# First MLP pair by plain products, block sums between products, and w_down's transfers spread: one change to a decoder-layer kernel

## The chip, the core and the metric

The kernel runs on one core of a Trainium2 chip. It is one program for a whole decoder layer: SEQ = 1024 tokens, model width 1024, MLP width 2816, everything in float32. The metric is the device time of one execution in microseconds (us), as a median over runs.

## The reference, cut to what matters

The change touches the second half of the layer: the residual after the mixers, the norm, the causal ConvFFN MLP.

```python
h = h + rmsnorm(mixed @ w_o, norm_mix_post)
f = rmsnorm(h, norm_ffn_pre) @ w_up                 # 1024 x 1024 @ 1024 x 5632
f = causal_dwconv(f, conv_ffn) + conv_ffn_b         # 3 taps over tokens, per channel
f_gate, f_val = jnp.split(f, 2, axis=-1)            # 2816 channels each
f = (jax.nn.gelu(f_gate) * f_val) @ w_down          # 2816 x 1024
h = h + rmsnorm(f, norm_ffn_post)
```

Ahead of it lie the input projection, a gated DeltaNet mixer and a sparse-attention mixer, and behind it a gated per-layer embedding. The change leaves those alone.

## The kernel before

**Number format.** Every float32 product is done as three matmuls of a rounded format (float32r): a value is split into a high half (ScalarE copies and rounds it) and a low half (another engine subtracts the high half from the value). `hl` does a split and `mm3` the three matmuls. So a 128-row block of K costs three matmuls, and a "product" below, 512 deep and 512 wide, is 4 x 3 = 12 matmuls of 512 columns.

**Blocks of tokens.** `ffn` goes through the eight blocks of 128 tokens. `product(t, half)` multiplies a block with w_o, three blocks ahead of its use. `post` norms the result, adds `x` and gives `h` (stored as `h1d`); the block is normed again and `turned` transposes it on TensorE and splits it into `mx`. `mx[kh, th]` holds half kh of the 1024 inputs for half th of the tokens; for the second half of the tokens, `mx[0, 1]` holds B12 - B11, not B12 itself.

**The MLP pairs.** w_up is used in 22 pairs of 128 gate and 128 value channels; class `UpProjection` holds them. A pair is a 2x2 block product done with seven products instead of eight (Winograd's form of Strassen): its four weight blocks a11, a12 (gate) and a21, a22 (value) meet B11, B12, B21, B22 and three combinations T2, T3, T4. Products 1, 2, 3 and 5 need `mx` alone. Products 6, 7 and 4 need T2, T3, T4. `sums` makes the weight sums s1 to s4 on VectorE, `ring` splits a weight block into one of four slots (high half on ScalarE, low half on GpSimd), `gate_lo` and `gated` do the convolution taps and the GELU, `keep` stores the activations and, for every second pair, four block sums of two pairs (GpSimd), for `down` is a block product of the same kind. `stores` issues those transfers later, on SyncE's queue.

**The start.** Products 1 and 2 of pairs 0 and 1 run between the last blocks (`under`). Then `rest` calls `combine`, which makes T2, T3 and T4 from `t2s` and `mx` on VectorE, GpSimd and ScalarE, and goes on with product 6 of pair 0.

**The order** within an engine's queue is written by a scheduler at build time, from the order of the program, its own cost model, and the buffers that are free. `behind(ins)` ties each instruction in its block to come after `ins` on that engine's queue. A tile with a tag shares its `bufs` slots with every tile of the same tag, so a new one waits until the older one has been read.

**down** runs seven block products, each eleven steps of 12 matmuls over four banks. `run` issues the loads of w_down's quarters (`load_w`) at given steps, on SyncE's queue, behind the load of that step's activations (`araw`).

## Time and profile before

| | us |
|---|---|
| median of 3 runs (1950.59 to 1951.98) | 1951.12 |
| profiled execution | 1951.64 |
| span of its instructions | 1949.9 |
| TensorE busy | 1839.1 |
| VectorE busy | 1224.2 |
| ScalarE busy | 920.3 |
| GpSimd busy | 711.6 |

The span runs from the first to the last instruction that the profile shows; the execution's own time is 1.7 us longer. Busy time counts an instruction from start to end. Matmuls overlap: one of 512 columns lasts 0.39 us in the rows, but starts come closer than that, so the cost of a matmul is read from the distance of the starts. The engines are PE (TensorE), PEld (its weight loads), DVE (VectorE), ACT (ScalarE), POOL (GpSimd) and SP (SyncE, which issues transfers).

### The profile page before, as it was taken

How to read it: one execution, taken by the hardware profiler on the slowest of the kernel's cores; microseconds unless marked ns; L12 is line 12 of the kernel's file. 1: busy time of each engine (PE TensorE's matmuls, PEld its weight loads, DVE VectorE, ACT ScalarE, POOL GpSimd, SP SyncE). 2: the span in 40 equal slices, each digit the busy share in tenths (PEclk: the TensorE clock that was granted, in tenths of full speed). 3: DMA queues.
4: the chain of work that ended last, by engine and by line, in shares of the span. 5: the costliest groups of instructions: out<-in, count | busy, mean ns of one | idle time of the engine just before them, and what ended most of it. 6: DMA issues, size and time to landing. Idle time of an engine off the chain costs nothing.

```text
span 1949.9 us, 25814 instructions
## 1 busy us (share of the span) xinstructions
PE 1839.1 (94%) x9247; PEld 1528.1 (78%) x9247; DVE 1224.2 (63%) x2347; ACT 920.3 (47%) x1816; POOL 711.6 (36%) x537
## 2 busy tenths in 40 slices
PE   7999989999999999999889949999999999999998
PEld 7888778888888887778778837787787877777786
DVE  4448934432277667766694587777677764868643
ACT  4344223323276667766663334444454544446432
POOL 2132212223122112321162166666666664555200
PEclk9999989999999999999999969999999999999999
DMA  5133333333311010200073212232323257246201
GB/s 166 33 95 103 101 83 93 97 87 95 100 28 34 28 39 28 71 23 23 22 248 121 97 55 81 92 103 88 122 83 103 92 184 259 72 146 208 88 33 43
DMA packets 182622, 178.67 MB, mean 92 GB/s; under 512 B 27549, under 2 KB 133342, under 8 KB 182494
## 3 DMA queue, kind: packets, MB, share of 16 engines
q1 hardware_dynamic: 180272, 170.33, 27.8%
q10 hardware_dynamic: 2222, 6.69, 0.9%
q8 instruction: 73, 1.20, 0.3%
q14 instruction: 55, 0.45, 0.1%
HBM read 132.65 MB, written 44.34 MB: 91 GB/s over the span
## 4 chain that ended last, share of the span: by engine, by line
PE 34%; DVE 5%; POOL 4%; issue 3%; ACT 2%; DMA 2%; SPq 0%; POOLq 0%; ACTq 0%; DVEq 0%
PE q L345 3%; PE q L347 3%; PE q L346 3%; PE n L345 2%; PE n L347 2%; PE n L346 2%; PE pg L347 2%; PE pg L346 2%; PE pg L345 2%; PE pwo L347 1%; PE pwo L345 1%; PE pwo L346 1%; POOL whl L313 1%; POOL wdhl L313 1%; DMA araw<-acts 1%
## 5 line engine op out<-in xcount | busy, mean ns | idle before, releaser
L345 PE MATMUL pj<-uh,whi 128*128 128x512 f32 x640 | 260.0, 407 | 6.0 <-DVE y L524 3.7
L347 PE MATMUL pj<-uh,wlo 128*128 128x512 f32 x640 | 255.2, 399 | 0.0
L346 PE MATMUL pj<-ul,whi 128*128 128x512 f32 x640 | 255.2, 399 | 0.0
L313 POOL TENSOR_TENSOR wlo<-raw,whi 128x1024 fp32r<-128x1024 f32 x48 | 117.3, 2446 | 310.5 <-ACT whi L324 266.6
L313 POOL TENSOR_TENSOR whl<-s,whl 128x512 fp32r<-128x512 f32 x88 | 131.3, 1500 | 57.2 <-ACT whl L1344 57.2
L345 PEld LDWEIGHTS pj<-uh,whi 128*128 128x128 f32 x640 | 121.5, 190 | 33.3 <-ACT yz L562 2.8
L347 PEld LDWEIGHTS pj<-uh,wlo 128*128 128x128 f32 x640 | 121.3, 190 | 29.0
L346 PEld LDWEIGHTS pj<-ul,whi 128*128 128x128 f32 x640 | 121.8, 190 | 25.8
L313 POOL TENSOR_TENSOR whl<-raw,whl 128x512 fp32r<-128x512 f32 x66 | 105.8, 1605 | 58.1 <-ACT whl L1344 55.5
L313 POOL TENSOR_TENSOR wdhl<-wd,wdhl 128x512 fp32r<-128x512 f32 x66 | 98.9, 1507 | 76.1 <-ACT wdhl L1344 74.8
L313 DVE TENSOR_TENSOR whl<-araw,whl 128x512 fp32r<-128x512 f32 x77 | 84.4, 1103 | 56.5 <-ACT whl L1344 54.0
L1226 ACT ACTIVATE Pt<-Pt,nm 128x640 f32<-128x640 f32 (+7 forms) x128 | 93.0, 729 | 36.6 <-DVE nm L1224 36.2
L345 PE MATMUL q<-mxh,whl 128*128 128x512 f32 x264 | 103.8, 396 | 4.1 <-ACT u L106 2.8
L1256 DVE TENSOR_TENSOR Tl<-pt,Th 128x512 fp32r<-128x512 f32 (+1 forms) x152 | 92.4, 616 | 22.1 <-ACT Th L1255 17.9
L346 PE MATMUL q<-mxl,whl 128*128 128x512 f32 x264 | 103.5, 392 | 0.0
L347 PE MATMUL q<-mxh,whl 128*128 128x512 f32 x264 | 102.9, 392 | 0.2 <-POOL whl L313 0.2
L1255 ACT ACTIVATE Th<-pt 128x512 fp32r<-128x512 f32 (+1 forms) x152 | 78.5, 538 | 43.7 <-PE po L1259 33.7
L324 ACT ACTIVATE whi<-raw 128x1024 fp32r<-128x1024 f32 x48 | 50.5, 1052 | 82.8 <-PE pj L346 54.1
L1252 PE MATMUL pt<-ident,Pt 128*128 128x128 f32 x528 | 84.6, 280 | 5.0 <-DVE Tl L1256 3.2
L1294 POOL TENSOR_TENSOR tm<-tm 128x128 f32<-128x128 f32 x32 | 14.7, 459 | 197.2 <-DVE tm L1292 157.4
L126 DVE SCALAR_TENSOR_TENSOR yg<-c,cv,yg 128x511 f32<-128x511 f32 (+1 forms) x88 | 82.0, 936 | 1.0 <-ACT yg L123 0.9
L1344 ACT ACTIVATE whl<-s 128x512 fp32r<-128x512 f32 x88 | 54.7, 624 | 55.8 <-PE n L347 44.1
(533 smaller groups left out, 5181.8 us busy)
## 6 DMA issues: line engine op xcount, KB each, us to landing
raw<-in_w_up SPq DMA_DIRECT2D x44, 512.0 KB
raw<-in_w_in SPq DMA_DIRECT2D x40, 512.0 KB
araw<-acts SPq DMA_DIRECT2D x35, 512.0 KB
acts<-sd SPq DMA_DIRECT2D x44, 256.0 KB
gates_d<-yz SPq DMA_DIRECT2D x40, 256.0 KB
acts<-yv SPq DMA_DIRECT2D x33, 256.0 KB
gt<-gates_d SPq DMA_DIRECT2D x32, 256.0 KB
wd<-in_w_down SPq DMA_DIRECT2D x7, 1024.0 KB
```

The costliest lines, as they stand in the source:

```text
L126: self.body.nc.vector.scalar_tensor_tensor(y, src, w, y, ALU.mult, ALU.add)
L313: return eng.tensor_sub(lo, src, hi.bitcast(F32)).ins
L324: nc.scalar.activation(hi, raw, AF.Copy)
L345: nc.tensor.matmul(ps, lh, rh, start=start, stop=False, skip_group_check=more)
L346: nc.tensor.matmul(ps, lh, rl, start=False, stop=False, skip_group_check=more)
L347: nc.tensor.matmul(ps, ll, rh, start=False, stop=stop, skip_group_check=more)
L1226: nc.scalar.activation(Pt[:, hh, 0:nk], Pt[:, hh, 0:nk], AF.Exp, scale=2.0 ** -(h0 + hh + 1), bias=nm[:, br, hh:hh + 1], accum_out=rs[:, b ...
L1252: nc.tensor.transpose(pt[:, b, hh], Pt[:, hh, (b0 + b) * P:(b0 + b + 1) * P], self.ident)
L1255: nc.scalar.activation(Th[:, 0:m], pt[:, 0:m], AF.Copy)
L1256: nc.vector.tensor_sub(Tl[:, 0:m], pt[:, 0:m], Th[:, 0:m].bitcast(F32))
L1294: nc.gpsimd.tensor_add(tm[:, 0], tm[:, 0], tm[:, 1])
L1344: self.nc.scalar.activation(hi, src, AF.Copy)
```

## The change

In `rest` and its helpers: pair 0 is computed by eight plain products. `plain` does a21 x B11 and a22 x B21 (lower token half of the value channels), `plain_rest` adds a11 x (B12 - B11), a12 x B22, and the same for a21, a22, cut into two halves of 256 tokens. `combine` becomes `open` (tiles) and `turn` (one T, some blocks), all of it on VectorE, called in a written order with `behind`. T2's first three blocks are made when the last block of tokens has been normed.

In `ffn`: `h` is written into `x`, the normed block into `h1`; a block is turned ahead of the product that follows three blocks later; the pools are cut anew.

In `keep`: block sums are put on a list (`todo`), and the loop does one at a time on GpSimd between two products (`between`); after the last pair three of four go to VectorE.

In `down`: the loads of w_down's quarters are issued at other steps, two of them in the third product.

```diff
@@ class UpProjection
+    def times(self, w, i, ps, first, part=slice(0, 512)):
+        bh, bl = self.B[i]
+        for k in range(4):
+            self.body.mm3(ps[:, part], w[:, 0, k], w[:, 1, k], bh[:, k, part], bl[:, k, part], first and k == 0,
+                          k == 3, not first)
+    def plain(self, p):
+        p.R, p.N = self.bank("r"), self.bank("n")
+        self.times(self.ring(p.a[1][0]), 1, p.R, True)
+        p.rr = self.sp.tile([P, 512], F32, name="rr", tag="sd1")
+        self.body.nc.scalar.activation(p.rr, p.R, AF.Copy)
+        self.times(self.ring(p.a[1][1]), 2, p.N, True)
+    def plain_rest(self, p):
+        ws = [(ps, i, self.ring(p.a[r][k])) for r, ps in enumerate((p.Q, p.R)) for k, i in enumerate((5, 3))]
+        for part in (slice(0, 256), slice(256, 512)):
+            for ps, i, w in ws:
+                self.times(w, i, ps, False, part)
+        p.c2 = self.up.tile([P, SEQ], F32, name="c2", tag="c2", bufs=1)
+        self.body.nc.scalar.activation(p.c2[:, 512:], p.R, AF.Copy)
...
-        s = [self.up.tile([P, 512], F32, name=f"sd{i}", tag=f"sd{i}") for i in range(1, 5)]
-        eng.tensor_add(s[0], a0[:, hi], a[:, hi])
-        eng.tensor_sub(s[1], s[0], a0[:, lo])
-        eng.tensor_sub(s[2], a0[:, lo], a0[:, hi])
-        eng.tensor_sub(s[3], a[:, lo], s[1])
-        for i in range(4):
-            self.store(3 + i, j, s[i])
+        s = [self.sp.tile([P, 512], F32, name=f"sd{i}", tag=f"sd{i}") for i in range(1, 5)]
+        self.todo = [(3, s[0], ALU.add, a0[:, hi], a[:, hi]), (4, s[1], ALU.subtract, s[0], a0[:, lo]),
+                     (5, s[2], ALU.subtract, a0[:, lo], a0[:, hi]), (6, s[3], ALU.subtract, a[:, lo], s[1])]
+        if p.n == NF - 1:
+            for eng in (self.body.nc.vector, self.body.nc.vector, self.body.nc.gpsimd, self.body.nc.vector):
+                self.block_sum(j, eng)
+    def block_sum(self, j, eng):
+        i, dst, op, x, y = self.todo.pop(0)
+        eng.tensor_tensor(dst, x, y, op)
+        self.store(i, j, dst)
...
+    def turn(self, t2s, n, us):
+        body, ve = self.body, self.body.nc.vector
+        for u in us:
+            t2 = t2s[u]
+            c, t = slice(u * P, u * P + P), t2
...
+            if n == 3:
+                ve.tensor_sub(t, t2, b[0])
+                ve.tensor_sub(t, t, b[1])
+            elif n == 4:
+                ve.tensor_sub(t, b[0], t2)
+                ve.tensor_add(t, t, b[1])
+            lo = body.hl(*[m[:, :, c] for m in self.T[n]], t, ve)
+        return lo
...
-        self.sums(a, (1, 2, 3, 4))
-        self.combine(t2s)
-        self.sums(b, (1, 2))
-        self.p6(a)
-        self.gate_lo(a)
+        self.plain_rest(a)
+        self.load(2)
+        with body.behind(*ends):
+            self.turn(t2s, 2, range(3, 4))
+            self.sums(b, (1, 2))
+            self.turn(t2s, 3, range(2))
+            self.sums(b, (3,))
+            t3 = self.turn(t2s, 3, range(2, 4))
         self.p6(b)
-        self.p5(a)
-        self.sums(b, (3, 4))
-        self.p7(a)
-        self.c22(a)
+        with body.behind(t3):
+            nc.vector.tensor_add(a.c2[:, 0:512], a.N, a.rr)
+            self.sums(pairs[2], (1, 2))
+            self.gate_lo(a)
+        self.start(pairs[2])
         self.p5(b)
-        self.p3(a)
-        self.p4(a)
-        self.gated(a)
-        self.keep(a)
-        self.gate_lo(b)
-        self.load(2)
+        with body.behind(t3):
+            self.sums(b, (4,))
+            t4 = self.turn(t2s, 4, range(4))
         self.p7(b)
+        with body.behind(t4, self.copied):
+            self.sums(pairs[2], (3,))
+            self.gate_lo(b)
+            self.gated(a)
+            self.keep(a)
+        self.p3(b)
         self.c22(b)
-        self.sums(pairs[2], (1, 2, 3))
-        self.start(pairs[2])
         self.p4(b)
-        self.p3(b)
...
+            def between():
+                if self.todo:
+                    with body.behind(self.lo):
+                        self.block_sum(last, nc.gpsimd)
             self.second(p)
+            if n % 2:
+                between()
...
                 self.start(nxt)
+            between()
             self.p4(p)
+            between()
             self.p3(p)
+            between()
@@ class Body, ffn
-        under = {5: ((up.start, 0),), 6: ((up.second, 0), (up.start, 1)), 7: ((up.second, 1),)}
+        under = {5: ((up.start, 0), (up.second, 0)), 6: ((up.plain, 0), (up.start, 1)), 7: ((up.second, 1),)}
...
-            self.post(pw.pop(t), wpost, x, h1, f"h1{t}", h1)
-            nc.sync.dma_start(h1d[t], h1)
-            if 3 <= t + 3 < NT:
-                for half in range(2):
-                    product(t + 3, half)
+            self.post(pw.pop(t), wpost, x, h1, f"h1{t}", h1, x)
+            nc.sync.dma_start(h1d[t], x)
...
+            nc.scalar.activation(h1, x, AF.Square, accum_out=ss)
+            r = self.rstd_of(ss, 1, 1.0 / DM, "hn")
+            normed = nc.vector.scalar_tensor_tensor(h1, x, r, wpre, ALU.mult, ALU.mult).ins
+            if t == 7:
+                with self.behind(normed):
+                    up.turn(t2s, 2, range(3))
+            ends = turned(t, h1)
+            if t + 3 < NT:
+                for half in range(2):
+                    product(t + 3, half)
@@ class Body, down
-            ((0, ((0, 0, npre, 8), (0, 0, 8, hf))), (2, ((1, 0, 0, 4),)), (4, ((1, 0, 4, 8),)), (6, ((1, 0, 8, hf),)),
-             (8, ((1, 1, 0, 4),))))
+            ((0, ((0, 0, npre, 8), (0, 0, 8, hf))), (4, ((1, 0, 0, 4),)), (8, ((1, 0, 4, 8),))))
...
-        run(product(1, b21, M, True), ((0, ((1, 1, 4, 8),)), (2, ((1, 1, 8, hf),)), (4, ((0, 1, 0, 4),)),
-                                       (6, ((0, 1, 4, 8),)), (8, ((0, 1, 8, hf),))))
+        run(product(1, b21, M, True), ((0, ((1, 0, 8, hf),)), (2, ((1, 1, 0, 4),)), (4, ((0, 1, 0, 4),)),
+                                       (6, ((1, 1, 4, 8),)), (8, ((0, 1, 4, 8),))))
...
         for j in product(6, b22, Z, True):
+            with self.behind(self.araw):
+                if j < 2:
+                    load_w(1 - j, 1, 8, hf)
```

## Rows read from the trace of the kernel before

**Rows 1.** Table by stretches: length, busy time (instructions) per engine, clock, DMA, GB/s.
```profile
core 0: us, PE busy (x) PEld busy (x) DVE busy (x) ACT busy (x) POOL busy (x), PEclk, DMA share, GB/s
1127.00:1175.00 48.00, 22.34 (x75) 16.43 (x74) 40.43 (x47) 17.09 (x30) 32.37 (x18) 0.68 0.14 41
1175.00:1260.00 85.00, 80.37 (x344) 65.10 (x343) 61.65 (x67) 39.40 (x60) 53.84 (x37) 0.98 0.29 95
1260.00:1745.00 485.00, 469.38 (x2014) 378.47 (x2013) 345.90 (x371) 222.12 (x352) 302.05 (x204) 0.99 0.36 119
```

**Rows 2.** Waits of PE, 1113.5 to 1260 us: total us, times, longest.
```profile
PE q L345 <- ACT whl L1344: 12.6, 1, 12.6
PE q L347 <- POOL whl L313: 8.6, 3, 5.7
PE pT_hn L1390 <- DVE x L1432: 3.0, 1, 3.0
PE q L345 <- ACT u L106: 2.8, 1, 2.8
```

**Rows 3.** Waits of PE, 1300 to 1750 us.
```profile
PE q L347 <- POOL whl L313: 8.6, 4, 2.2
PE dm L345 <- ACT whl L1344: 1.8, 1, 1.8
```

**Rows 4.** Chain that ended last, 1100 to 1260 us: start, length, what.
```profile
1113.94 0.89 PE pT_hn L1390 x8
1114.84 3.38 DMA x<-in_x
...
1128.80 1.63 DVE x L1432
```

**Rows 5.** Timeline, first block of tokens: its first square, its last norm instruction.
```profile
1044.93 0.58 ACT L1304 ACTIVATE h<-pwo 128x512 f32<-128x512 f32 x1
...
1052.32 1.27 DVE L1432 SCALAR_TENSOR_TENSOR x<-h,rb_hn,wpre 128x1024 f32<-128x1024 f32 x1
```

**Rows 6.** Timeline of PE: two matmuls of 512 columns, twelve apart.
```profile
1097.24 0.39 PE L345 MATMUL pwo<-w_oh,mxh 128*128 128x512 f32 x1
...
1099.96 0.39 PE L345 MATMUL pwo<-w_oh,mxh 128*128 128x512 f32 x1
```

**Rows 7.** Timeline of PE: matmuls of 256 columns, four apart.
```profile
883.64 0.28 PE L1259 MATMUL po<-Th,vst 128*128 128x256 f32 x1
...
884.10 0.28 PE L1259 MATMUL po<-Th,vst 128*128 128x256 f32 x1
```

**Rows 8.** Timeline of PE: the first matmul that reads T2.
```profile
1145.06 0.79 PE L345 MATMUL q<-T2h,whl 128*128 128x512 f32 x1 [12.55 <-ACT whl L1344]
```

**Rows 9.** The stretch in which T2 to T4 are made: table, groups of DVE, POOL.
```profile
1131.70:1166.10 34.40, 13.15 (x41) 9.02 (x39) 30.62 (x35) 12.38 (x22) 24.40 (x13) 0.63 0.06 17
...
L221 DVE TENSOR_TENSOR t<-t,mxh 128x512 f32<-128x512 f32 x4 | 6.9, 1751 | 3.6 <-POOL T3l L313 3.6
...
L222 DVE TENSOR_TENSOR t<-t,mxl 128x512 f32<-128x512 f32 x4 | 2.7, 677 | 0.0
...
L313 POOL TENSOR_TENSOR whl<-s,whl 128x512 fp32r<-128x512 f32 x5 | 13.3, 2685 | 5.0 <-ACT whl L1344 5.0
```

**Rows 10.** Table by stretches: two of those at the slow clock.
```profile
1129.70:1157.00 27.30, 8.19 (x22) 5.95 (x22) 22.29 (x28) 8.79 (x16) 18.20 (x9) 0.50 0.06 19
...
1409.60:1413.00 3.40, 3.40 (x10) 2.59 (x9) 0.00 (x0) 0.93 (x2) 1.15 (x1) 0.52 0.43 145
```

**Rows 11.** Timelines of POOL and PE around one burst of block sums.
```profile
1405.32 1.27 POOL L201 TENSOR_TENSOR sd<-sd,yv 128x512 f32<-128x512 f32 x1
1406.56 1.71 POOL L313 TENSOR_TENSOR whl<-s,whl 128x512 fp32r<-128x512 f32 x1
...
1408.32 0.50 PE L347 MATMUL q<-T2h,whl 128*128 128x512 f32 x1 [2.16 <-POOL whl L313]
```

**Rows 12.** Table by stretches: 20 us of the first product of `down`.
```profile
1600.00:1620.00 20.00, 20.00 (x87) 16.07 (x86) 6.70 (x7) 7.46 (x13) 15.54 (x11) 1.00 0.94 328
```

More of the change, by code (lines that the diff above doesn't have):

```diff
@@ L53, in __init__ @@
         self.B = {1: body.mx[0, 0], 2: body.mx[1, 0], 3: body.mx[1, 1], 5: body.mx[0, 1]}
-        self.pairs, self.nring, self.later = {}, 0, []
+        self.pairs, self.nring, self.later, self.todo = {}, 0, [], []
     def ring(self, src, eng=None):
@@ L281, in rest @@
         ues.close()
+        ses.close()
         tes.close()
@@ L1296, in nsa_back, with post @@
         return at
-    def post(self, parts, wbc, res, dst, name, junk):
+    def post(self, parts, wbc, res, dst, name, junk, out=None):
         nc, w = self.nc, DM // len(parts)
@@ L1310, in post @@
         r = self.rstd_of(ss[:, 0:1], 1, 1.0 / DM, name)
-        nc.vector.scalar_tensor_tensor(dst, dst, r, res, ALU.mult, ALU.add)
+        nc.vector.scalar_tensor_tensor(dst if out is None else out, dst, r, res, ALU.mult, ALU.add)
     def resident(self, pool, w, ks, engs=None, place=None):
@@ L1368, in ffn @@
         cv = wq.tile([P, 4, 2 * NF], F32, name="cv")
-        wp = self.pool(self.wes, "woB")
+        wb = self.pool(self.wes, "woB")
         for ks, tag in (((4, 5), "raw"), ((6,), "hi"), ((7,), "lo")):
-            self.wo += self.resident(wp, "w_o", ks, place=(self.wp, tag))
+            self.wo += self.resident(wb, "w_o", ks, place=(self.wp, tag))
+        up = UpProjection(self, bank, cv)
+        ses, nes, tes = ExitStack(), ExitStack(), ExitStack()
+        up.sp = self.pool(ses, "up0", side="right", own=True)
+        wp = self.pool(nes, "norms", side="right")
         wpost = wp.tile([P, DM], F32, name="wpost")
@@ L1376, in ffn @@
         pw, t2s = {}, []
-        up = UpProjection(self, bank, cv)
         def product(t, half):
```

58 lines of the change are left out of this document (22 added, 36 removed).

## The prediction

> **What bounds the kernel now.** I read the page's busy times first: TensorE is the fullest engine by far, so only its gaps and its slow clock can be worth much. The table by stretches then says where they lie [rows 1]. From 1127 to 1175 us, where the normed activations are done and the MLP pairs begin, TensorE is busy for 22.3 of 48 us and its mean clock is 0.68; from 1175 to 1260 us another 4.6 us are idle; the 485 us of the pair loop and the first w_down products lose only 15.6 us. So the change has 25.7 + 4.6 = 30.3 us of idle time in front of it, and a little more behind.
>
> The view of waits names what ends each gap [rows 2]: 12.6 us for ScalarE's high half of the first weight that meets T2, 8.6 us in three waits for GpSimd's low half of such a weight (the longest 5.7), 3.0 us for the last normed block, 2.8 us for a copy out of bank q. All of the first stall is one story: pair 0 can go on only with `p6`, which needs T2, `s2` and a split weight, and `combine` puts 28 element-wise instructions and the splits in front of it on three engines. In the pair loop four waits of the same line give 8.6 us, and a wait for a split activation in product 1 of `down` gives 1.8 [rows 3].
>
> The chain that ended last shows why the last block is late [rows 4]: after product 7 come, at 1113.94, the transposes of block 4, they free an `x` buffer, the next `x` block is fetched (3.4 us), then VectorE makes `h`; the normed last block starts at 1128.8, 15 us after product 7. Block 0, which waits for no buffer, takes 1052.32 + 1.27 - 1044.93 = 8.7 us from first square to normed block [rows 5].
>
> **The first pair by plain products.** Pair 0 does eight products instead of seven. A product is 12 matmuls of 512 columns; twelve lie 1099.96 - 1097.24 = 2.72 us apart [rows 6], so the extra one costs 2.7 us. Four of the eight are cut into halves of 256 columns: 96 matmuls for 48. The nearest rows have 256 columns and a new weight each, four steps in 884.10 - 883.64 = 0.46 us, 0.115 us each [rows 7]: 96 x 0.115 = 11.0 against 48 x 0.227 = 10.9. Bounds: 0, and 10.9 more if a half lasted as long as a whole. Those rows are of the same shape, so I take 0.2, 2.9 in all.
>
> What it buys is order. Pair 0 no longer needs T2, T3 or T4. After product 7 (1113.9, or 1114.8 since block 4's 0.89 us of transposes now go ahead of it) TensorE has: transposes of three blocks (2.8), eight products of pair 0 (22.0), and for pair 1 products 1 and 2 (5.4) before anything needs T2: until 1114.8 + 30.2 = 1145.0. The halves of 256 columns also let half of `plain_rest` run before the last block is turned. T2 is then asked for when it is first used now, at 1145.06 [rows 8], but with its splits and `s2` of pair 1 ahead of all else on VectorE. I expect no wait there.
>
> The order in `post` also changes: `h` is written into `x`, whose buffer is freed by the store of `h1d`, not by transposes queued behind a product, so the 3.4 us fetch leaves the chain and block 7 can be normed at about 1114.8 + 8.7 = 1123.5, before its transposes' turn on TensorE at about 1130 (1114.8, two blocks' 1.8, five products' 13.6). The 3.0 us go. If the store is slower than the transposes were, 3 us come back; I take 0 to 3, and 0.
>
> **What is late next: T3 and T4.** Every split and subtraction of T2 to T4 now goes to VectorE, tied in order. Behind block 7's transposes (1130.5) I count until T4 is whole: 5 for the turned block, 1 for T2, 3 sums of pair 1, 12 for T3, the sum for `c2`, 2 sums of pair 2, 3 of `gate_lo`, 1 more sum, 12 for T4: 40 instructions. Before, the same kind of work took 30.62 us for 35, 0.875 us each [rows 9]: 40 x 0.875 = 35.0, so T4 at 1165.5. Without products that need T4 TensorE has pair 1's 6, 5, 7, 3 and pair 2's first (13.6) until 1158.6, and if the order written by the scheduler takes pair 2's 2, 6 and 5 before, until 1166.8. That leaves 0 to 7 us idle; I take 4. Bounds are the two sizes of one 128x512 subtraction in the same stretch, 677 and 1751 ns [rows 9]: T4 at 1157.6, no wait, or at 1200.5, some 38 us. I add 3 us for the small waits of 1.5 to 2.8 us for copies and banks, whose kind stays. Seven idle us remain.
>
> GpSimd pays as well: its splits of weights took 2.685 us each in that stretch [rows 9], against 1.71 in a quieter place [rows 11]. A product needs one split in 2.72 us, so at that size they would just keep up.
>
> The Trainium skill, GPSIMD Engine Reference, section Key points, says that GpSimd shares its SBUF interfaces with VectorE and contends with VectorE instructions that have two SBUF inputs. That speaks against giving VectorE seven more splits while GpSimd goes on splitting weights; the trace agrees, with one shape at 677 and 1751 ns [rows 9], and by the rule at its worst the time would be that of the third rival.
>
> **The clock.** A stretch at the 1.2 GHz level loses half of what TensorE is busy in it. Around the first stall the granted clock is 0.50 from 1129.7 to 1157 with 8.19 us busy: 4.1 us [rows 10]. Two stretches of 3.4 us, like the one shown there, follow gaps in this region, at most 1.7 each and 3.2 together. In all 7.3. With seven us of smaller gaps left I let 2.5 remain.
>
> Sum for the first part: 30.3 + 7.3 - 2.9 - 7 - 2.5 = 25.2 us gained. Ends: 10 (T4 15 us later than taken) and 33 (no gap left).
>
> **Block sums between products.** Four sums of an odd pair now stand together on GpSimd: in the timeline a sum of 1.27 us at 1405.32 lies ahead of the split that product 6 needs, that split takes 1.71 us until 1408.27, and TensorE goes on at 1408.32 after 2.16 us idle [rows 11]. Four such waits are the 8.6 us of [rows 3]; a fifth is most of the 2.9 that [rows 2] leave beside the longest, and stands in the first part. After one of the four the clock falls for 3.4 us: 1.7 more [rows 10]. Spread behind single splits, each sum delays one split by 1.3 to 1.7 us, and four weight slots let splits run ahead; GpSimd is busy for 302 of 485 us [rows 1], so there is room. I take 10 of 10.3; bounds 4 (two waits stay) and 10.3. The eleventh group of sums, after the last pair, goes mostly to VectorE: 3 x 0.68 = 2.0 us, or 5.3 at the long size. VectorE is busy for 6.70 of 20 us there [rows 12], which hides it; if the first splits of `down` came behind it, up to 2 us. I take nothing.
>
> **w_down's transfers.** From 1600 to 1620 us the DMA engines are busy for 0.94 of the time at 328 GB/s [rows 12], and the activations of product 1 come late: 1.8 us idle, and one more slow stretch of 3.4 us (1.7) right after. Each product lasts 11 x 2.72 = 30 us; the change moves two transfers out of the first and two from the second into the third. Every one still has at least 6 x 2.72 = 16 us before its rows are used. I take 3 of 3.5; bounds 0 and 3.5.
>
> **Sum.** The profiled execution took 1951.6 us (span 1949.9 and 1.7 around it), 0.5 above the median of the runs shown. 25 + 10 + 3 = 38 us: 1913.6 on that execution, 1913 as a median.
>
> **Rivals.**
> 1. VectorE becomes the bound of the first part. Its 40 instructions take 1.2 us each, between the two sizes, T4 is whole at 1178.5, and with the work owed behind it (`gate_lo`, `gated`) TensorE idles 15 to 25 us instead of 7. For it: the tie puts all of T4 before `gated`, and the dense run on VectorE makes GpSimd's splits late too. Against: the mean of 0.875 already holds 24.4 us of GpSimd work in 34.4. Time 1923 to 1934.
> 2. The sums still delay a split, in other places: GpSimd has four splits and four sums, about 12 us, in four products' 10.9 us. Then 5 to 8 of the 10 us stay away: 1918 to 1922 with the rest as forecast.
> 3. Contention at its worst: all 40 at 1.75 us. T4 at 1200.5, 34 to 42 us idle and 4 us more of slow clock: the first part loses 9 to 17 instead of gaining; with 13 behind, 1947 to 1955.
> 4. Slower: the sums, tied behind splits, push every split that follows. There are 44, about 1.4 us each, 62 us; it turns the balance if more than 38 of these are seen by TensorE, 61%. For it: a stall of 2.16 us stands behind one burst of sums already. Against: that is 2.16 of about 11 for the two bursts between stalls. At 75% the time is 1960.
> 5. The scheduler keeps the old order nearly everywhere and only the extra product is new: 1951 to 1954. The 30 us gap speaks against it, since pair 0 cannot need T2 any more.
>
> **Chances.** The forecast, with 1904 to 1922 as its own range, 0.59; rival 1 0.21; rival 2 0.09; rival 3 0.04; rival 4 0.04; rival 5 0.03. Range 1902 to 1935: its lower end is a first part without any gap (33 us), and it takes in rivals 1 and 2, 0.89 in all. A difference of 0.2% (3.9 us) is about what a measurement of this kernel can tell from no change. Faster: the first three cases and half of rival 3, 0.91. Same: the other half, and two thirds of rival 5, 0.04. Slower: the rest, 0.05.
>
> **What would show it.** Right: no idle gap over 3 us between 1113 and 1145; T2's first product at about 1145 at the full clock; one product more of work in the first pair, 96 matmuls of 256 columns near 0.115 us apart; no wait for a weight's low half in the pair loop; DMA share under 0.8 in the first product of `down`. Wrong: a long wait for T3h or T4h or for a sum `s` at 1150 to 1180 (rivals 1 and 3), POOL waits of `q` or `m` in the loop (2 and 4), or a wait for a `wd` block in products 2 and 3 of `down`.

## The result, and the profile after

The changed kernel takes 1929.88 us (median; 1925.03 to 1935.9) against 1951.55 for the kernel before on the same chip: a ratio of 0.9891, 95% interval 0.9874 to 0.9907. It is faster by 1.1%, 21.7 us; 38 were forecast. The time lies in the range of 1902 to 1935, but above the 1904 to 1922 that the forecast itself had.

The profiled execution took 1925.03 us (span 1923.3). Five events are the same in both programs: the first w_o product (`pwo`), the first product of `down` (`dq`), its second (`dm`), its third (`dz`), and the first product behind it (`pg`). The view of one tile gives the first and the last start of its matmuls; here are three such rows of the kernel after (durations min/median/max in ns, then the two starts in us).

```profile
L394 PE MATMUL pwo<-w_oh,mxh x128: 389/389/477, 1020.3 to 1111.4; 128*128 128x512 f32 x128
...
L394 PE MATMUL dq<-wdhl,whl x132: 392/397/628, 1562.6 to 1728.2; 128*128 128x512 f32 x132
...
L394 PE MATMUL dz<-wdhl,whl x44: 392/396/472, 1626.8 to 1656.0; 128*128 128x512 f32 x44
```

The same rows of the kernel before begin at 1022.9, 1590.0 and 1657.3; the other events were read in the same way. So the span divides like this:

| stretch | before | after | difference | forecast |
|---|---|---|---|---|
| start to first `pwo` | 1022.9 | 1020.3 | -2.6 | 0 |
| `pwo` to `dq`: norms, first pair, pair loop | 567.1 | 542.3 | -24.8 | -35.2 |
| `dq` to `dm`: first product of `down` | 33.0 | 31.5 | -1.5 | -3 with the next |
| `dm` to `dz`: second product | 34.3 | 32.7 | -1.6 | |
| `dz` to `pg`: the other five products | 174.6 | 178.5 | +3.9 | 0 |
| `pg` to the end | 118.0 | 118.0 | 0 | 0 |

The first row is not the change's: nothing in it was edited, and over the thirteen profiles of the changed kernel and its variants below the first `pwo` starts between 1016.9 and 1027.8 us. So variants are compared below by their medians and, more finely, by these stretches, one profile each. Ten microseconds of the forecast are missing between `pwo` and `dq`, and 3.9 were lost where nothing was forecast.

The table by stretches of the kernel after, where [rows 1] showed that of before:

```profile
core 0: us, PE busy (x) PEld busy (x) DVE busy (x) ACT busy (x) POOL busy (x), PEclk, DMA share, GB/s
1127.00:1175.00 48.00, 44.71 (x233) 38.19 (x232) 47.41 (x60) 24.07 (x38) 23.74 (x15) 0.93 0.19 56
1175.00:1260.00 85.00, 79.23 (x338) 63.86 (x337) 73.45 (x73) 40.45 (x60) 58.09 (x37) 0.98 0.29 96
1260.00:1580.00 320.00, 314.64 (x1366) 254.90 (x1365) 246.53 (x261) 150.95 (x231) 213.27 (x146) 1.00 0.34 113
1580.00:1640.00 60.00, 58.22 (x247) 46.02 (x247) 33.68 (x33) 25.90 (x46) 29.41 (x21) 1.00 0.66 233
1640.00:1745.00 105.00, 98.36 (x404) 77.08 (x403) 76.41 (x79) 52.12 (x91) 55.87 (x34) 0.97 0.40 127
```

In the first stretch TensorE went from 22.34 to 44.71 us busy in 48, and its mean clock from 0.68 to 0.93; VectorE, the engine that paid, stands at 47.41. The last stretch is where `down` loses: 6.6 us idle, and the clock below 1 again. TensorE's waits (total, times, longest), first from 1113.5 to 1260 us as in [rows 2], then from 1260 to 1571, then from 1571 to 1760 (together the place of [rows 3]):

```profile
PE n L394 <- DVE c L179: 3.8, 2, 2.5
PE q L394 <- ACT r L106: 3.0, 2, 2.8
PE n L396 <- POOL whl L362: 2.2, 2, 1.7
...
PE q L394 <- ACT r L106: 4.6, 14, 1.1
PE q L396 <- POOL whl L362: 0.7, 1, 0.7
...
PE dq L395 <- POOL wdhl L362: 6.1, 3, 5.7
PE dz L394 <- DVE facc L1554: 1.6, 1, 1.6
PE dq L396 <- DVE whl L362: 0.7, 1, 0.7
```

The four waits for GpSimd's low half in the loop (8.6 us) are gone, and so is that for a late activation block (`dm`). Two kinds take their place: fourteen short ones for ScalarE's copy `r`, and a single one of 5.7 us in product 4 of `down`. That one is the largest gap of the kernel after, and it stands in lines that the change doesn't touch (L1567 and L1568 were L1507 and L1508). The timeline around it, VectorE, ScalarE, GpSimd and TensorE:

```profile
1673.41 0.63 ACT L1393 ACTIVATE whl<-araw 128x512 fp32r<-128x512 f32 x1 [4.24 <-DMA araw<-acts]
...
1673.95 0.61 ACT L1393 ACTIVATE wdhl<-wdT 128x512 fp32r<-128x512 f32 x1
...
1674.64 11.48 POOL L362 TENSOR_TENSOR wdhl<-wdT,wdhl 128x512 fp32r<-128x512 f32 x3 [4.10 <-ACT wdhl L1393]
...
1675.23 0.67 DVE L362 TENSOR_TENSOR whl<-araw,whl 128x512 fp32r<-128x512 f32 x1
1675.83 0.68 DVE L1567 TENSOR_TENSOR wd<-wd,wd 128x512 f32<-128x512 f32 x1
...
1681.85 0.68 DVE L1568 TENSOR_TENSOR wd<-wd,wdT 128x512 f32<-128x512 f32 x1
...
1683.70 0.80 PE L395 MATMUL dq<-wdhl,whl 128*128 128x512 f32 x1 [5.72 <-POOL wdhl L362]
```

The POOL row holds three subtractions; the chain that ended last gives the first of them 9.02 us:

```profile
1670.54 4.06 issue
...
1674.64 9.02 POOL wdhl L362
```

The shortest of these subtractions in product 4 takes 1.27 us. Here VectorE runs thirteen of its own back to back from 1674.62 to 1682.53, each still at 0.68, and GpSimd ends 1.13 us after the last of them. Two causes offer themselves: the transfer that comes late in the first row, with ScalarE's copies queued behind it, or VectorE's unbroken run. The rows weigh them: a split of 1.27 us begun at 1674.64 would have ended at 1675.91, and TensorE had work until 1683.70 - 5.72 = 1677.98. So the late transfer alone would have cost no wait; it set the moment at which the split began. The kernel before has such a row too, the longest of its splits in product 4:

```profile
L313 POOL TENSOR_TENSOR wdhl<-wdT,wdhl x11: 1283/1702/4230, 1688.8 to 1716.1; 128x512 fp32r<-128x512 f32 x11
```

Its 4.23 us begin at 1716.07, when five subtractions of VectorE's run are left, and end 1.14 after the last of them; TensorE waited 0.31 us for it.

### The profile page after: what moved, and what is told of

Its sections match the earlier page's. It is cut to its first block, busy times and chain, and to the rows that moved or that the text cites. A ratio compares the mean times of both kernels' runs of the same rounds, so it can differ in the third digit from the quotient of the medians.

```text
span 1923.3 us, 25903 instructions
## 1 busy us (share of the span) xinstructions
PE 1834.8 (95%) x9307; PEld 1524.8 (79%) x9307; DVE 1242.5 (65%) x2353; ACT 919.2 (48%) x1817; POOL 700.2 (36%) x527
## 5 line engine op out<-in xcount | busy, mean ns | idle before, releaser
L362 POOL TENSOR_TENSOR whl<-s,whl 128x512 fp32r<-128x512 f32 x84 | 119.5, 1425 | 70.8 <-ACT whl L1393 69.0
L362 POOL TENSOR_TENSOR whl<-raw,whl 128x512 fp32r<-128x512 f32 x71 | 114.6, 1621 | 62.6 <-ACT whl L1393 62.0
L362 DVE TENSOR_TENSOR whl<-araw,whl 128x512 fp32r<-128x512 f32 x77 | 89.8, 1173 | 54.9 <-ACT whl L1393 54.8
L394 PE MATMUL q<-mxh,whl 128*128 128x512 f32 (+1 forms) x272 | 105.9, 394 | 7.7 <-ACT r L106 7.7
L1305 DVE TENSOR_TENSOR Tl<-pt,Th 128x512 fp32r<-128x512 f32 (+1 forms) x152 | 92.5, 616 | 21.7 <-ACT Th L1304 17.3
L396 PE MATMUL q<-mxh,whl 128*128 128x512 f32 (+1 forms) x272 | 105.1, 387 | 0.7 <-POOL whl L362 0.7
L395 PE MATMUL q<-mxl,whl 128*128 128x512 f32 (+1 forms) x272 | 105.3, 387 | 0.0
L152 DVE SCALAR_TENSOR_TENSOR yg<-c,cv,yg 128x511 f32<-128x511 f32 (+2 forms) x88 | 76.9, 875 | 2.1 <-ACT yg L149 1.8
L152 DVE SCALAR_TENSOR_TENSOR yv<-c,cv,yv 128x1023 f32<-128x1023 f32 (+1 forms) x44 | 65.7, 1492 | 15.7 <-ACT yv L149 13.4
```

The lines of the kernel that those rows point to most:

```text
L152: self.body.nc.vector.scalar_tensor_tensor(y, src, w, y, ALU.mult, ALU.add)
L362: return eng.tensor_sub(lo, src, hi.bitcast(F32)).ins
L394: nc.tensor.matmul(ps, lh, rh, start=start, stop=False, skip_group_check=more)
L395: nc.tensor.matmul(ps, lh, rl, start=False, stop=False, skip_group_check=more)
L396: nc.tensor.matmul(ps, ll, rh, start=False, stop=stop, skip_group_check=more)
L1305: nc.vector.tensor_sub(Tl[:, 0:m], pt[:, 0:m], Th[:, 0:m].bitcast(F32))
```

## The experiments

Each is the changed kernel with the edit shown, measured beside the kernel before on the same chip, whose own medians there lie between 1949.42 and 1951.55 us; the stretches are from its profile. From `pwo` to `dq` six of them run the same code (changed kernel, again, old_loads, half_burst, wd_first, all_vec), in 541.9 to 543.2 us, so a difference of about 1.3 us in that column says nothing by itself.

| run | median us | ratio to before, 95% | `pwo` to `dq` | `dq` to `dm` | `dz` to `pg` |
|---|---|---|---|---|---|
| changed kernel | 1929.88 | 0.9891, 0.9874 to 0.9907 | 542.3 | 31.5 | 178.5 |
| again | 1928.36 | 0.9889, 0.9876 to 0.9901 | 541.9 | 31.1 | 177.7 |
| old_loads | 1933.66 | 0.9912, 0.9899 to 0.9925 | 542.0 | 35.7 | 179.1 |
| burst_sums | 1934.6 | 0.9921, 0.9909 to 0.9933 | 546.3 | 31.6 | 178.1 |
| half_burst | 1920.66 | 0.9852, 0.983 to 0.9873 | 543.2 | 31.4 | 170.0 |
| wd_first | 1926.25 | 0.9878, 0.9858 to 0.9899 | 541.9 | 31.1 | 177.6 |
| split_T | 1933.38 | 0.9908, 0.9889 to 0.9927 | 545.6 | 31.4 | 179.6 |
| r_first | 1924.58 | 0.9863, 0.9841 to 0.9884 | 540.1 | 31.1 | 178.9 |
| half_p1 | 1916.01 | 0.9823, 0.98 to 0.9846 | 537.1 | 31.2 | 169.5 |
| burst_p1 | 1920.42 | 0.9845, 0.9824 to 0.9866 | 531.3 | 31.7 | 178.7 |
| all_vec | 1922.54 | 0.9848, 0.9827 to 0.9869 | 542.4 | 31.1 | 172.2 |
| best | 1914.37 | 0.9825, 0.9798 to 0.9853 | 535.9 | 31.0 | 169.9 |
| burst_best | 1910.11 | 0.9786, 0.9768 to 0.9805 | 532.0 | 31.1 | 170.4 |

### The same kernel again, and the old load steps

The first run changes nothing. The second puts w_down's loads back to their steps of before:

```diff
-            ((0, ((0, 0, npre, 8), (0, 0, 8, hf))), (4, ((1, 0, 0, 4),)), (8, ((1, 0, 4, 8),))))
...
-        run(product(1, b21, M, True), ((0, ((1, 0, 8, hf),)), (2, ((1, 1, 0, 4),)), (4, ((0, 1, 0, 4),)),
...
-            with self.behind(self.araw):
-                if j < 2:
-                    load_w(1 - j, 1, 8, hf)
```

(with the two lists of the kernel before in their place).

> The changed kernel once more, for its spread and a second profile. Theory A (a dense run of VectorE instructions in product 4 of down keeps GpSimd's split waiting, and by how much differs from execution to execution): median 1926 to 1933, spread over 5 us, and a wait of TensorE for a split of GpSimd between 1675 and 1700 us of a size that differs from the first profile's 5.7 us. Theory B (the spread comes from the stages ahead of the MLP, where both kernels have the same queues): the wait is again 5.7 us within 0.3, and the start of the w_o products differs by several us.

> The changed kernel with w_down's transfers at the steps of before. Theory A: the long wait in product 4 stays (3 to 6 us), and the wait at the start of product 1 comes back with its slow clock, 3.3 us: 1930 to 1935. Theory C (the transfers moved into the third product make the activations of product 4 late, and this is the wait): the wait in product 4 is gone, 5.7 us and some 3 us of slow clock come back against 3.3 us lost: 1921 to 1926.

The repeat has the same 5.71 us wait in product 4, and its span is 3.6 us longer because the first `pwo` starts 5.3 us later: what differs between these two profiles comes from the stages ahead, as theory B said. With the old load steps that wait stays at 5.71, so the spread transfers are not its cause. They cost 4.6 us in `down`'s first product instead (35.7 against 31.1): TensorE waits there again, and the clock falls behind it. TensorE's waits of this kernel from 1566 to 1760 us, and the stretch behind the new one:

```profile
PE dq L395 <- POOL wdhl L362: 5.9, 2, 5.7
PE dq L394 <- ACT whl L1393: 2.9, 1, 2.9
```

```profile
1597.50:1601.50 4.00, 3.72 (x9) 3.00 (x10) 2.33 (x3) 1.90 (x4) 1.28 (x1) 0.57 0.89 279
```

### Block sums in one burst

```diff
-        if p.n == NF - 1:
+        if p.n < NF - 1:
+            for _ in range(4):
+                self.block_sum(j, self.body.nc.gpsimd)
+        else:
```

> The changed kernel with the four block sums of a pair at once on GpSimd, as before; the last pair's stay as changed. The prediction's theory (spread sums are worth 8.6 us of waits and 1.7 of slow clock in the loop): 8 to 11 us slower than the changed kernel, with waits of 2.2 us for a weight's low half after every fourth pair. Rival (the new waits for the copy out of bank q, 4.6 us where there were 0.9, take part of it back): 4 to 7 us slower, and with the sums in one burst the waits for the copy fall to about 1 us.

The stretch from `pwo` to `dq` grows by 4.4 us against the repeat (546.3 against 541.9), the median by 6.2. So spreading the sums is worth some 4 to 6 us in this kernel, not 10, although all four waits of before are back (8.4 us in the loop). The rival had this size. What was gained on them was partly handed on to the waits for `r`: in the loop 1.6 us in five here, 4.6 us in fourteen with the sums spread. The edit does more than its lines say: the traces show that the scheduler also wrote another order of products in part of the loop. So the 4.4 us are the price of the burst and of that order together.

### Half of product 4's block sums moved

```diff
         for j in product(4, t2, Q, False):
             with self.behind(up.lo):
                 nc.vector.tensor_sub(b12[:, j], b22[:, j], b12[:, j])
-                nc.vector.tensor_sub(b21[:, j], b21[:, j], t2[:, j])
...
-        run(product(3, b11, Q, False))
+        for j in product(3, b11, Q, False):
+            with self.behind(up.lo):
+                nc.vector.tensor_sub(b21[:, j], b21[:, j], t2[:, j])
```

These sums are VectorE's subtractions of w_down's blocks, not the block sums of the pairs.

> The changed kernel with half of VectorE's subtractions of product 4 of down done in product 3, where VectorE has little to do. Theory A: the long wait in product 4 shrinks below 1 us and its slow clock goes; 6 to 9 us faster than the changed kernel (1919 to 1924), and the spread of the runs falls to about 2 us. Theory B or C: the wait in product 4 stays over 3 us, and the time is the same within 2 us.

With eleven of VectorE's instructions out of product 4 the wait is gone, and the five products take 170.0 us: 7.7 less than in the repeat, and 4.6 less than in the kernel before. GpSimd's splits of product 4 (min/median/max in ns) in the changed kernel and, in the second fence, here:

```profile
L362 POOL TENSOR_TENSOR wdhl<-wdT,wdhl x11: 1273/1295/9012, 1658.3 to 1691.9; 128x512 fp32r<-128x512 f32 x11
```

```profile
L362 POOL TENSOR_TENSOR wdhl<-wdT,wdhl x11: 1281/1498/1753, 1662.6 to 1686.6; 128x512 fp32r<-128x512 f32 x11
```

None is over 1.8 us any more. This shows that the wait hangs on VectorE's load in that product, not yet how. The spread of the runs did not fall to about 2 us, as theory A had it: they lie between 1917.29 and 1930.33.

### ScalarE's queue, or VectorE beside GpSimd

In the first of two edits the weights' copy and split are issued ahead of the activations' ones in each step. In the second, product 4's split moves from GpSimd to VectorE, which then has more work than before.

```diff
# wd_first
+                w = thp.tile([P, 2, 512], F32R, name="wdhl", tag="wdhl", bufs=3)
+                self.wlo = self.hl(w[:, 0], w[:, 1], B(j) if callable(B) else B[:, j], nc.gpsimd)
                 a = up.ring(raw[:, j % 2], nc.vector)
-                w = thp.tile([P, 2, 512], F32R, name="wdhl", tag="wdhl", bufs=3)
-                self.wlo = self.hl(w[:, 0], w[:, 1], B(j) if callable(B) else B[:, j], nc.gpsimd)
# all_vec
-        def product(src, B, banks, first):
+        def product(src, B, banks, first, eng=None):
...
-                self.wlo = self.hl(w[:, 0], w[:, 1], B(j) if callable(B) else B[:, j], nc.gpsimd)
+                self.wlo = self.hl(w[:, 0], w[:, 1], B(j) if callable(B) else B[:, j], eng or nc.gpsimd)
...
-        for j in product(4, t2, Q, False):
+        for j in product(4, t2, Q, False, nc.vector):
```

> The changed kernel, but in every step of the down projection the copy and the split of the weights' block are issued ahead of those of the activations' block, so that on ScalarE no weight copy stands behind an activation copy whose transfer is late. If the 5.7 us wait in product 4 comes of that queue (ScalarE waits 4.2 us for the transfer, the weight copy stands behind it, GpSimd's split starts late), the wait falls below 1 us, the slow clock after it goes, and the kernel gains 4 to 8 us (about 1922). If it comes of VectorE alone, whose three two-input instructions a step hold GpSimd's split up, a wait of at least 4 us stays and the time is within 2 us of the changed kernel's.

> The changed kernel, but in product 4 of the down projection the low half of the weights' block is subtracted on VectorE, which then has four subtractions a step and GpSimd none. If GpSimd's split is held up because it runs beside VectorE's subtractions, and each stretches the other, then VectorE's four run at about 0.68 us each (2.7 us a step, as long as TensorE's twelve matmuls), the 5.7 us wait goes or falls below 2.5 us in all, and the kernel gains 3 to 7 us although VectorE has more to do. If VectorE simply has too much work in that product, eleven more subtractions make it 5 to 8 us later: waits of 8 us or more, and a slower kernel.

With the order in each step turned round the 5.7 us wait stays as it was, the five products take 177.6 us, and the longest split is 9.03 us. This doesn't clear the late transfer. The edit only moves a weight's copy to stand behind the activations' copy of the step before: that copy waits 5.10 us for its transfer until 1671.27, the weight's copy follows at 1671.81, and the split begins at 1672.50. But the same working as above holds here: at 1.27 us it would have ended at 1673.77, and TensorE had work until 1675.88. With all four subtractions of a step on VectorE the five products take 172.2 us, 5.5 less than in the repeat, and the median is 5.8 us lower. The waits of TensorE from 1630 to 1700 us in that kernel, and two of VectorE's groups from 1663 to 1694 (busy us, mean ns of one, idle before):

```profile
PE dz L394 <- DVE facc L1554: 2.2, 1, 2.2
PE dq L395 <- DVE wdhl L362: 1.3, 1, 1.3
```

```profile
L1568 DVE TENSOR_TENSOR wd<-wd,wdT 128x512 f32<-128x512 f32 x11 | 7.5, 685 | 0.0
...
L362 DVE TENSOR_TENSOR wdhl<-wdT,wdhl 128x512 fp32r<-128x512 f32 x11 | 7.5, 685 | 0.0
```

VectorE did eleven instructions more and was done sooner (26 us from its first to its last one in the product, against 33), for now each takes 0.685 us on average, where in the changed kernel six take 1.77 to 1.79. So in these rows the two engines don't work beside each other on these instructions: one holds the other up, and a dense run of VectorE held GpSimd's 9 us split up until it ended.

### Low halves of T3 and T4 on GpSimd

Is VectorE, at 47.41 of 48 us, the bound of the first part, so that it should give work back?

```diff
-            lo = body.hl(*[m[:, :, c] for m in self.T[n]], t, ve)
+            lo = body.hl(*[m[:, :, c] for m in self.T[n]], t, body.nc.gpsimd if n > 2 and u % 2 == 0 else ve)
```

> The changed kernel, but the low halves of blocks 0 and 2 of the combinations T3 and T4 are subtracted on GpSimd, not on VectorE (four instructions). If VectorE is the bound of the first part (busy 47.4 of 48 us), it gains four times 0.68 us, the waits for ScalarE's r and VectorE's c (2.8, 1.3 and 2.5 us) shrink by about that and the kernel gains 2 to 4 us. If GpSimd beside VectorE only stretches both, the waits for GpSimd's splits grow by 2 to 6 us and the time is the same or up to 4 us longer. I expect the second, weakly: within 2 us of the changed kernel.

The stretch grows by 3.7 us against the repeat (2.8 of them are more idle time of TensorE: 17.0 against 14.2 us), the longest wait for ScalarE's `r` from 2.8 to 3.9 us, and those for VectorE's `c` from 3.8 us in the changed kernel to 5.1. The waits for GpSimd's splits, which I expected to grow, are 2.2 us in both. Giving four subtractions away saves VectorE only 2.3 us of busy time from 1127 to 1175 (45.15 against 47.41), while GpSimd's grows by 4.2 (27.93 against 23.74). My lean (within 2 us) was too mild, and its way was another. GpSimd's four added instructions in this kernel, from 1125 to 1180 us, and one VectorE group that did not change its work:

```profile
L362 POOL TENSOR_TENSOR T4l<-t,T4h 128x512 fp32r<-128x512 f32 x2 | 3.4, 1692 | 1.3 <-ACT T4h L1393 1.3
L362 POOL TENSOR_TENSOR T3l<-t,T3h 128x512 fp32r<-128x512 f32 x2 | 2.6, 1296 | 5.6 <-ACT T3h L1393 5.6
...
L257 DVE TENSOR_TENSOR t<-t,mxl 128x512 f32<-128x512 f32 x4 | 4.8, 1220 | 0.0
```

That last group took 950 ns on average in the changed kernel.

### ScalarE's copy r ahead of T4's copies

The longest wait of the first part after stands at 1157 us. ScalarE's and TensorE's timeline in the changed kernel:

```profile
1152.08 0.63 ACT L1393 ACTIVATE T4h<-t 128x512 fp32r<-128x512 f32 x1 [0.51 <-DVE t L257]
...
1154.38 0.63 ACT L1393 ACTIVATE T4h<-t 128x512 fp32r<-128x512 f32 x1 [0.67 <-DVE t L257]
1156.06 0.63 ACT L1393 ACTIVATE T4h<-t 128x512 fp32r<-128x512 f32 x1 [1.04 <-DVE t L257]
1156.59 0.58 ACT L106 ACTIVATE r<-q 128x512 f32<-128x512 f32 x1
...
1157.23 0.80 PE L394 MATMUL q<-mxh,whl 128*128 128x512 f32 x1 [2.79 <-ACT r L106]
```

The copy of `r` waits for nothing of its own; it stands in ScalarE's queue behind copies of T4 that wait for VectorE, and T4 itself is not asked for before 1178.

```diff
-            t4 = self.turn(t2s, 4, range(4))
+            self.turn(t2s, 4, range(1))
+        with body.behind(t3, self.copied):
+            t4 = self.turn(t2s, 4, range(1, 4))
```

> The changed kernel, but the last three blocks of T4 are tied behind ScalarE's copy of r as well, so that this copy doesn't stand behind their copies in ScalarE's queue. If the 2.8 us wait of TensorE at 1157 us comes of that queue, it falls below 0.5 us; T4 is then whole some 5 us later, still ahead of its product at 1178 us, and the kernel gains 2 to 4 us (the clock's loss there goes too). If VectorE, idle until the copy is through, falls behind instead, the wait comes back at T4's product or at VectorE's c and the time stays within 1.5 us.

The wait for `r` falls to 0.7 us in three, but one of 2.9 appears for ScalarE's copy of a weight (`m`). The stretch shortens by 1.8 us against the repeat. Both halves of what was written came in part: the queue was the cause of that wait, and most of the room that it left was taken by the next one.

### Product 1 behind product 5 in the loop

In the order that the scheduler writes, product 1 of the next pair mostly runs ahead of product 5, and only two matmuls stand between product 5 and product 3, which writes the bank that ScalarE copies as `r`. The edit ties product 1 behind product 5 (`self.mm` is the last matmul that `mm3` issued):

```diff
             self.p5(p)
+            mm5 = body.mm
             self.c22(p)
             if nxt:
                 self.sums(nxt, (1, 2, 3))
-                self.start(nxt)
+                with body.behind(mm5):
+                    self.start(nxt)
```

It was run with the half of product 4's sums moved (half_p1), and with the sums in one burst (burst_p1).

> The version with half of product 4's block sums moved to product 3, and in the loop over pairs the next pair's product 1 is tied behind product 5, so that twelve matmuls stand between product 5 and product 3, which needs the bank that ScalarE copies after product 5. If the loop's 4.6 us of waits for ScalarE's copy r come of the two matmuls that stand there now, they fall below 1 us, the stretch from the first w_o product to the first product of the down projection falls from 542 to about 538 us, and the time comes to about 1917. If the wait only moves (to GpSimd's split, 8.6 us in the kernel before), the stretch stays at 541 to 544 and the time at about 1920.5.

> The changed kernel with the four block sums in one burst on GpSimd, as in the kernel before, and the loop's product 1 tied behind product 5. With the changed order of products the spread of the sums was worth 4.2 us (stretch from the first w_o product to the down projection 546.3 against 542.1). If the waits for ScalarE's copy r had taken the rest of the 10 us that I had put on the sums, the burst costs more once those are gone: the stretch is 545 to 548 here, against 537.1 with the sums spread, a price of 8 to 11. If the two are independent, the stretch is 541 to 542 and the price stays at 4.

With the sums spread the stretch falls from 543.2 to 537.1 and the waits for `r` in the loop from fourteen to one of 0.7 us, as the first expectation of half_p1 said. Of these 6.1 us 1.7 are a stretch at the slow clock that half_burst has in its loop (0.50 from 1328.4 to 1331.8, 3.40 us of work) and half_p1 and the repeat don't; against the repeat's 541.9 the fall is 4.8. That so much came of waits of 4.6 us, while a new one for VectorE's `c` cost 2.1 in the loop, has a reason that the view of waits doesn't show. One of the fourteen in the changed kernel:

```profile
1343.85 0.39 PE L395 MATMUL q<-T2l,whl 128*128 128x512 f32 x1
1344.47 0.50 PE L394 MATMUL q<-mxh,whl 128*128 128x512 f32 x1 [0.23 <-ACT r L106]
1344.80 0.40 PE L395 MATMUL q<-mxl,whl 128*128 128x512 f32 x1
```

The wait is given as 0.23 us, counted from the end of the matmul before. But the starts lie 0.62 and 0.33 us apart, where 2.72 / 12 = 0.23 is usual in [rows 6]: 0.5 us are lost, twice what the view says, for the overlap of the matmuls was broken as well.

With the sums in one burst the stretch falls from 546.3 to 531.3: neither of the two expectations, 545 to 548 or 541 to 542. Here both have the same order of products in the loop, so up to `dq` nothing but the sums differs. In this order the burst is not dearer than the spread sums but 5.8 us cheaper. Two stretches of the loop, first with the sums spread (half_p1), then in one burst (burst_p1):

```profile
1327.80:1427.80 100.00, 98.59 (x434) 80.95 (x434) 88.54 (x85) 47.84 (x73) 68.72 (x45) 1.00 0.30 97
1427.80:1527.80 100.00, 99.30 (x438) 81.91 (x437) 84.48 (x83) 48.17 (x73) 72.88 (x49) 1.00 0.34 111
```

```profile
1324.10:1424.10 100.00, 100.00 (x442) 82.78 (x442) 77.05 (x85) 48.22 (x73) 70.93 (x49) 1.00 0.33 107
1424.10:1524.10 100.00, 100.00 (x443) 82.80 (x442) 79.39 (x87) 50.56 (x75) 68.63 (x48) 1.00 0.31 100
```

In the burst TensorE has no gap there at all, and in the first of each VectorE's 85 instructions take 77.05 us in place of 88.54. The timelines show one place where that arises: the product `yv` of a pair (L204). In half_p1 one of GpSimd's instructions runs beside it, a spread sum or a split:

```profile
1307.81 1.74 POOL L234 TENSOR_TENSOR sd<-yv 128x512 f32<-128x512 f32 x1
...
1308.33 2.31 DVE L204 TENSOR_TENSOR yv<-yg,yv 128x1024 f32<-128x1024 f32 x1
```

In burst_p1 GpSimd's next instruction is a sum that waits for that very product, so GpSimd stands still meanwhile:

```profile
1301.90 1.21 DVE L204 TENSOR_TENSOR yv<-yg,yv 128x1024 f32<-128x1024 f32 x1
...
1303.19 1.67 POOL L237 TENSOR_TENSOR sd<-yv 128x512 f32<-128x512 f32 x1 [1.76 <-DVE yv L204]
```

All fifteen of burst_p1 from 1270 to 1550 us, and then those of half_p1, in the view of that line (min/median/max in ns):

```profile
L204 DVE TENSOR_TENSOR yv<-yg,yv x15: 1210/1212/1214, 1283.3 to 1547.5; 128x1024 f32<-128x1024 f32 x15
```

```profile
L204 DVE TENSOR_TENSOR yv<-yg,yv x15: 1211/2311/2319, 1270.0 to 1539.8; 128x1024 f32<-128x1024 f32 x15
```

From 1280 to 1540 us TensorE is busy for 257.89 of 260 us in half_p1 and for all 260.00 in burst_p1, which is 2.1 of the 5.8 us. It waits there for VectorE's `c` in half_p1, in the view from 1277.8 to 1552.9 us, and for nothing in burst_p1:

```profile
PE n L396 <- DVE c L179: 2.1, 3, 0.7
```

The first part, ahead of the loop, holds another 2.1: in the 133 us that begin 106.7 us behind the first `pwo` TensorE is idle for 10.97 us in half_p1 and for 8.88 in burst_p1, with 6.4 and 4.0 us of waits for `c`. The remaining 1.6 were not taken apart. That a slower VectorE makes `c` late fits all this; no run tests it by itself.

### The edits together

best holds half_p1's edits and that of r_first; burst_best adds the sums in one burst.

> Three edits together on the changed kernel: half of product 4's block sums in product 3, the loop's product 1 behind product 5, and the last three blocks of T4 behind ScalarE's copy of r. By their stretches alone (8, 6 and 2 us) it comes to 1914 us, 1 to 3 us below the version with the first two. If the third only moves its wait once the loop's order is another, it is the same as that version, 1916.

> The version with three edits (half of product 4's block sums in product 3, the loop's product 1 behind product 5, the last three blocks of T4 behind ScalarE's copy of r), and the four block sums in one burst again. With product 1 behind product 5 the burst left the stretch from the first w_o product to the down projection at 531.3 us, the spread sums at 537.1: if that price of the spread sums holds here, the stretch falls from 535.9 to about 530 and the kernel comes to 1905 to 1910. If it was particular to that run, the stretch stays at 535 to 537 and the time at about 1914.

best came to 1914.37 us. Its stretch, 535.9, is 1.2 below half_p1's: in direction as written, but inside the 1.3 us that the same code differs by, and too small to be told by medians. burst_best came to 1910.11, with 532.0 us from `pwo` to `dq` (1905 to 1910 and 530 were expected): the price of the spread sums is there in this version too, 3.9 us, and r_first's edit brings nothing beside the burst (531.3 without it). It is the fastest version, 40.8 us under the kernel before and 18 to 20 under the changed kernel's medians. By stretches it is 8.2 us ahead of burst_p1 from the first `pwo` to `pg`, all of it behind `dz`.

## Why the prediction came out as it did

**The bound and the first part: right in kind, 4.4 us too high.** The idle time of 1127 to 1260 us was the place of the gain. As written there is no gap over 3 us from 1113 to 1145 (none over 0.5 until 1154), block 7 is turned at 1127.57 without a wait (1130 forecast), and T2's first product runs at 1142.57 without one. Behind 1260 us burst_sums loses about what the kernel before does (10.0 us idle against 9.6, and a stretch of 3.4 us at the slow clock in each), so before against burst_sums gives the worth of the part, 567.1 - 546.3 = 20.8 us; 25.2 were forecast. The terms that were off, in the changed kernel: idle time left, 7 forecast, 48.00 - 44.71 + 85.00 - 79.23 = 9.1 measured; slow clock left, 2.5 forecast, about 4.8 measured. The latter is two stretches at a granted clock of 0.50, from 1156.6 to 1163.4 us with 6.17 us of work and from 1211.2 to 1214.6 with 3.40, and half of 9.57 is 4.8. The 96 matmuls of 256 columns lie 0.120 us apart, not 0.115, 0.4 us more. The forecast's own sum with these sizes is 30.3 + 7.3 - 3.3 - 9.1 - 4.8 = 20.4. That this comes so near 20.8 is in part luck: burst_sums, from which the 20.8 come, has 11.8 us idle in this part and no slow clock, and by the same sum 22.5. No run takes the part's own edits (plain products, T2 to T4 on VectorE, the order in `post`) one from another.

**T4.** It was whole at 1162.7 (1165.5 forecast), and no product ever waited for it. The step "what is late next: T3 and T4" named the right engine and the wrong wait: VectorE's T4 delayed ScalarE's copies of it, and these the copy of `r` in ScalarE's queue. The idle time that I had put on T4 came from there and from VectorE's sums `c`. So rival 1, whose time (1923 to 1934) fits the result, is not what happened: its 15 to 25 us of idle time are 9.1.

**Block sums: the step that failed.** The range held the time; this term of the sum was mis-sized, 10 us forecast and 4 measured. I put 10 us on "block sums between products", reading [rows 11] as: four sums stand ahead of a split, so the 8.6 us of waits are theirs. The waits did go. But the spread brought 4.0 to 4.4 us, since product 3 then met the copy of `r`, and with product 1 tied behind product 5 the spread costs 3.9 to 5.8 us. The waits of [rows 3] had two conditions, the burst and the scheduler's order of products, and taking away either one ends them (but for one of 0.7 us in the changed kernel); the order is worth more. The price that I gave to a spread sum (one split later by 1.3 to 1.7 us, hidden by the slots) left out VectorE, which it holds up. Rival 2 had the size of the loss (5 to 8), by another way.

**w_down's transfers: right.** 3 us forecast, 1.5 + 1.6 measured, and 4.6 in the first product alone when the old steps are put back. The first sign that I gave, a DMA share under 0.8 in the first product, came out for the product as a whole, 0.75 against 0.92 before. In the 20 us that match those of [rows 12], ten behind its start, the share is 0.82 (0.94 there). Across the end of the product, from 1589.6 to 1609.6 us, it is 0.92.

**What the prediction did not have: product 4 of `down`, 3.9 us lost.** It was taken as untouched. All seven variants that left the work of product 4 on its engines show a wait of 5.7 us there (again, old_loads, burst_sums, wd_first, split_T, r_first, burst_p1), and the kernel before shows 0.5 in two waits for the same instructions. half_burst and all_vec show that it is VectorE beside GpSimd: less VectorE work, or GpSimd out of it, ends it. The hold itself was there before, 4.23 us of it, late in VectorE's run and at a cost of 0.31 us; in the changed kernel the split begins with thirteen of the run's subtractions ahead of it. What in the change moved that moment stays open: it is not the load steps and not the order of the pairs' sums, but the late transfer ahead of ScalarE's copies, which sets the moment, is in all eight profiles that have the wait (ScalarE waits 4.2 to 5.1 us for it) and was never taken away alone.

**Sum.** 25.2 + 10 + 3 forecast; 20.8 + 4.0 + 3.1 - 3.9 = 24.0 measured between the first `pwo` and the end, and 2.6 from the stages ahead in this profile.

**VectorE beside GpSimd.** The Trainium skill, GPSIMD Engine Reference, section Key points, was cited with the worst case (rival 3) as its price. In the first part the trace agrees in kind only: all that is idle there is 9.1 us, not the 34 to 42 of that rival. split_T agrees with it more clearly, 3.7 us for four instructions given back to GpSimd; so do half_burst, all_vec and the loop.

## What to carry to other kernels

A wait that names an engine may rest on two conditions, so before putting its whole length on one edit, ask which other wait stands just behind it on the same bank, and try the order of the products as well as that of the helpers. Count many short waits by the distances of the starts, not by the view's idle time, which gave 0.23 of 0.5 us here. When a scheduler writes the order, an edit of one engine's work can change another's order too, so compare the orders before giving a difference to the edit. In these runs element-wise work of two SBUF operands on VectorE and on GpSimd was one budget where the two ran at the same time: moving an instruction from one to the other helps only where the other is idle, and a dense run on VectorE must not be laid over a split that TensorE needs soon. A stage whose code is unchanged can still lose when what comes before it shifts; list the stages that run near their limit, and give each a term in the sum.

## What the runs showed of the hardware

In these traces VectorE's subtraction of two 128x512 blocks in SBUF mostly takes 0.68 us or about 1.78, and the difference of 1.1 is close to the 1.27 of GpSimd's shortest; with GpSimd out of product 4 it is 0.685 on average. The other way round the runs show no such ceiling: GpSimd's subtraction took 9.02 us, ending 1.13 after a run of thirteen VectorE instructions at 0.68, 9.00 to 9.06 in the seven other runs with that wait, and 4.23 beside a run of five in the kernel before. So sometimes the two take turns, and sometimes GpSimd got no turn as long as VectorE ran without a pause; what decides between the two is not shown. The Trainium skill, SBUF — State Buffer, section SBUF: two separate sides, says that the two engines' shared pair of ports is locked for a whole instruction and that the one that comes second blocks fully. The trace agrees, with 1.78 for 0.68; that one instruction is held up by thirteen in a row is told by the 9.02 us row and its like alone.

The granted clock fell in product 4 as it had in [rows 10]: 0.56 on average from 1683 to 1690 us in the changed kernel, so nearly all of it at the lower level of 1.2 GHz, right behind the 5.7 us gap, with 6.29 us of work in it.
